# SSD decays from masked sums, norms applied to mixed rows, and experts' latent rows added by halves, in a hybrid diffusion kernel

## The chip, the cores and the metric

One core of a Trainium2 chip runs the whole program. The metric is the device time in microseconds from start to end of one execution, as a median of several runs.

The engines are TensorE (PE, with its weight loads PEld), VectorE (DVE), ScalarE (ACT), GpSimd (POOL) and SyncE (SP). Here SP does little but issue DMAs. POOL issues some as well, and each of these two issues its transfers in its own order.

## The reference

Two layers run over 512 latent tokens and 256 context tokens of 1024 features. Each layer is a mixer (attention beside a bidirectional Mamba-2 SSD) and then a mixture of 16 experts. In the first layer the context tokens go through both as well; in the second they give only keys, values and states. What matters for the change:

```python
# SSD, one direction; chunks of 128 tokens, 2 groups x 4 heads of 64 (xs, dt, a, bm, cm)
xdt  = xs * dt
a_cs = cumsum(dt * a)                                   # within a chunk
seg  = a_cs[target] - a_cs[source]
decay = exp(where(tri, seg, -inf))
y_diag = einsum(cb[target, source] * decay, xdt)        # cb = C . B, one for each group
...                                                     # + states carried from chunk to chunk
y = y_f + flip(y_b)
# norms that feed the output projection
ssd  = gated_group_rmsnorm(y + d_res * xs, z, ssd_norm_w)   # 2 groups of 256 features
attn = rmsnorm(o, subln_w) * (1.0 - lam_init)               # each of 4 heads, 128 features
mix  = concatenate([attn, ssd]) @ w_out
x = x + g1 * mix
# experts: each takes its 64 best latent rows (and, in layer 0, its 32 best context rows)
ye = (silu(xe @ w_gate) * (xe @ w_up)) @ w_down * gate
x = x + g2 * zeros(n, d).at[idx].add(ye)
```

## The kernel before

**Stages.** Tokens lie in six tiles of 128 rows: tiles 0 to 3 are latents, 4 and 5 context. A layer runs through the input norm, the projection of the SSD's inputs with their convolution and the SSD's first group, the gate projection with the SSD's second group, four attention heads, the output projection with the routing, and the experts. By time in the profile (us) the first layer has its SSD at 60 to 240, attention at 240 to 430, output projection and routing at 430 to 600, experts at 600 to 1262; the second starts at 1262 and has its SSD at 1330 to 1480, attention at 1480 to 1640, output projection and routing at 1640 to 1765, experts at 1765 to 2412.

**Products.** Matrix products of the mixer are made in three passes of rounded fp32: every operand is split into a high part (an ACT copy) and a low part (value less high part, on DVE or POOL). Weights arrive as `raw` tiles in a ring of four and are split into `rt` by the class with `pull` and `flush`; its next `raw` is loaded when a low part is done.

**Order.** The Python code interleaves generators. `Slots.tick` advances each of them to its next `yield`; work behind `yield STEP` is put in later in the same tick, between the other generators' pieces, and work behind a plain `yield` in the next tick. PE's projection matmuls fill the ticks. Each engine's queue is in that written order, as are SP's and POOL's DMA issues; no queue is reordered on the chip.

**An SSD chunk** (`chunk`) handles 128 tokens of four heads, both directions at once: 12 chunks in the first layer, 8 in the second. `acs` holds the cumulative sums with the source token on the partition. `dt_part` also transposes them and stores them in DRAM (`acsd`), and each chunk loads the four heads' rows back, repeated over all 128 partitions, as `RB` (128 x 2 directions x 4 heads x 128 targets, 512 KB). So `RB` less the source's `acs` is the exponent. The lower and upper triangles are taken by multiplying `cb` by 0/1 masks (`cbm`), and one exponential serves both directions, of the smaller of the two exponents:

```python
self.ld(RB..., src[None].to_broadcast([P, 2, 512]))                       # SP
nc.gpsimd.tensor_tensor(tf, RB[:, 0], a[:, 0]..., op=OP.subtract)          # POOL, L1057
nc.vector.scalar_tensor_tensor(tf[:, h], RB[:, 1, h], a[:, 1, h:h + 1], tf[:, h], subtract, min)   # L1068, four
nc.scalar.activation(E[:, h], cbm[:, 0], AF.Copy, scale=d[:, 0, h:h + 1])  # L1064, four
nc.vector.scalar_tensor_tensor(E[:, h], cbm[:, 1], d[:, 1, h:h + 1], E[:, h], mult, add)           # L1072, four
nc.scalar.activation(tf, tf, AF.Exp)                                       # L1069
nc.vector.tensor_tensor(E, E, tf, op=OP.mult)                              # L1074
```

(`E` is named `G` in the trace; `d` is dt.) PE then multiplies `E` by the inputs (`yd`, L1081) and adds the carried states' part (`yo`). `state` makes those, with POOL's `xd` and `hstep`.

**Norms.** `rsqrt_steps` is 11 small DVE steps for 1/sqrt, most of them behind a `yield STEP`. For each chunk of the second group `z_out` squares and sums both groups of the gated row on ACT, goes through `rsqrt_steps` (`yrs`), multiplies by the norm's weights `wssd` and stores the row to `mixd` in DRAM. `attend` does the same for one head and one tile with `ors` and `wsub` (L1837) and stores `ob`; for the last head's latent tiles it transposes `ob` in place instead. `op_in` loads a tile of mixed rows (`mixin`) back, transposes it and splits it into `mT`; `op_tile` multiplies it by `w_out` in `OUT_ORDER`, and adds to x.

**Experts.** SP streams each expert's weights without pause. `moe` makes `yl`, 128 partitions x 512, for an expert's 64 latent rows: partition 32*j + r and half g hold quarter j (256 columns) of row 32*g + r. `add_rows` multiplies each half by gate and `G2` into a `ys` of 128x256 and adds it to x in DRAM with an indirect DMA on POOL (L1666), 128 pieces of 1 KB, so twice for an expert's latents. The context's 32 rows are one more such scatter. x is `xr` in the first layer and `out` in the second.

Of the kernel before, what the change touches and what calls it, by code (L numbers as in the profile page):

```python
# [37 lines left out]
R_N1, R_N2, R_CW, R_CB, R_L = 0, 8, 16, 40, 48  # L38
# [26 lines left out]
OUT_ORDER = (4, 5, 6, 7, 0, 1, 2, 3)  # L65
# [47 lines left out]
class Pieces:  # L113
# [7 lines left out]
    def fetch(self):  # L121
        f = next(self.todo, None)
        if f:
            self.raw.append(f(self.net.rawp.tile([P, 512], F32, tag="raw", name="raw", bufs=4)))

    def pull(self, hi, lo):
        self.turn += 1
        nc, x = self.net.nc, self.raw.pop(0)
        nc.scalar.copy(hi.bitcast(F32R), x)  # L129
        self.flush()  # L130
        self.low = (nc.gpsimd if self.turn % 2 or x.shape[-1] == 384 else nc.vector), lo, x, hi

# [9 lines left out]
class Net:  # L142
# [122 lines left out]
    def consts(self, p1):  # L265
# [8 lines left out]
        for l in range(2):  # L274
# [96 lines left out]
    def pieces(self, l):  # L371
# [22 lines left out]

        cbs = [cb for g in range(2) for _, cb in GROUP[g]]
# [7 lines left out]
        for b in range(2):  # L403
            yield from (cols(w_out, k, 512 * b) for k in OUT_ORDER)

# [285 lines left out]
    def layer_params(self, l, lp, p1, lam_init):  # L691
# [7 lines left out]
        self.wsub = lp.tile([P, P], F32, name="wsub")  # L699
        self.wssd = lp.tile([P, 512], F32, name="wssd")  # L700
# [9 lines left out]
        ld(self.wsub, bc(I["subln_w"][l:l + 1], P))  # L710
        ld(self.wssd, bc(I["ssd_norm_w"][l:l + 1], 512))
# [6 lines left out]

        nc.vector.tensor_scalar(self.wsub, self.wsub, 1.0 - lam_init, None, op0=OP.mult)
# [152 lines left out]
    def dt_part(self, l, p1, sp, psp):  # L872
# [62 lines left out]
        nc.scalar.activation(self.eacs, self.acs, AF.Exp)  # L935
        yield
# [102 lines left out]
    def chunk(self, l, g, c, G, sp, yp):  # L1039
# [7 lines left out]
        a, d, ea = dgh(self.acs), dgh(self.dt), dgh(self.eacs)  # L1047
# [840 lines left out]
```

## Time and profile before

| what | before |
|---|---|
| median of 3 runs | 2430.44 us (2430.13 to 2430.88) |
| the profiled execution's own time | 2429.65 us |
| its span, first to last instruction | 2427.9 us |
| mean granted clock of TensorE, of full speed | 0.964 |
| PE busy | 2175.3 us, 90% of the span |
| DVE busy | 995.3 us, 41% |
| ACT busy | 635.9 us, 26% |
| POOL busy | 480.9 us, 20% |

The shares are means over stages that differ. The page's second part cuts the span into 40 slices of 60.7 us: DMA stands at 9 tenths in the expert stages, and at 2 to 3 in the first layer's SSD slices, where DVE is at 7 to 9. What a change in a stage can be worth is read there.

### The profile page before, as it was taken

How to read it: one execution, taken by the hardware profiler on the slowest of the kernel's cores; microseconds unless marked ns; L12 is line 12 of the kernel's file. 1: busy time of each engine (PE TensorE's matmuls, PEld its weight loads, DVE VectorE, ACT ScalarE, POOL GpSimd, SP SyncE). 2: the span in 40 equal slices, each digit the busy share in tenths (PEclk: the TensorE clock that was granted, in tenths of full speed). 3: DMA queues.
4: the chain of work that ended last, by engine and by line, in shares of the span. 5: the costliest groups of instructions: out<-in, count | busy, mean ns of one | idle time of the engine just before them, and what ended most of it. 6: DMA issues, size and time to landing. Idle time of an engine off the chain costs nothing. (4 is left out here: it accounts for less than half of the span.)

```text
span 2427.9 us, 55950 instructions
## 1 busy us (share of the span) xinstructions
PE 2175.3 (90%) x23460; PEld 1335.8 (55%) x23460; DVE 995.3 (41%) x3088; ACT 635.9 (26%) x1739; POOL 480.9 (20%) x584
## 2 busy tenths in 40 slices
PE   6898988998999999999987988989799999988775
PEld 4677787785445455455444667887543333333332
DVE  5789589873111111111116787887611111111010
ACT  4334467521111111111113443565111010101000
POOL 4464233100111101101103464241000001000001
PEclk9999999999999999999998998999899999999998
DMA  7322723678999999999994325324999999999997
GB/s 255 85 76 83 267 63 99 207 249 330 393 403 405 390 401 393 398 395 399 394 388 122 92 58 192 111 71 150 361 370 414 408 411 408 414 409 409 409 412 275
DMA packets 234759, 702.46 MB, mean 289 GB/s; under 512 B 30860, under 2 KB 88412, under 8 KB 234508
## 3 DMA queue, kind: packets, MB, share of 16 engines
q1 hardware_dynamic: 220428, 681.43, 72.6%
q0 software_dynamic: 14080, 17.46, 3.9%
q8 instruction: 185, 3.03, 0.5%
q14 instruction: 66, 0.54, 0.1%
HBM read 675.05 MB, written 23.76 MB: 288 GB/s over the span
## 5 line engine op out<-in xcount | busy, mean ns | idle before, releaser
L1490 PE MATMUL gl<-gw,xeT 128*32 128x512 f32 (+1 forms) x8192 | 655.6, 466 | 62.9 <-DMA gw<-w_up 62.7
L1490 PEld LDWEIGHTS gl<-gw,xeT 128*32 128x32 f32 x8192 | 277.7, 111 | 441.9 <-issue 404.3
L1529 DVE SCALAR_TENSOR_TENSOR th<-th,gl 128x256 f32<-128x256 f32 (+1 forms) x96 | 37.5, 391 | 702.9 <-ACT th L1528 702.9
L1536 PE MATMUL yl<-rt,hl 128*32 128x256 f32 x4080 | 247.5, 380 | 13.6 <-PE gl L1490 9.2
L1528 ACT ACTIVATE th<-gl 128x256 f32<-128x256 f32 (+1 forms) x96 | 35.1, 367 | 774.3 <-PE gl L1490 767.7
L171 PE MATMUL pacc<-rt,H 128*128 128x384 f32 (+1 forms) x768 | 206.3, 351 | 4.5 <-ACT V L1719 2.2
L1536 PEld LDWEIGHTS yl<-rt,hl 128*32 128x32 f32 x4080 | 134.1, 110 | 117.8 <-issue 16.0
L1666 POOL DMA_INDIRECT out<-ys,sidx x32 | 49.5, 1546 | 710.7 <-DVE ys L1665 599.1
L1665 DVE SCALAR_TENSOR_TENSOR ys<-yl,gate,G2l 128x256 f32<-128x256 f32 x64 | 28.0, 479 | 361.3 <-PE yl L1536 361.3
L1573 PE MATMUL gc<-gw,xeT 128*32 128x352 f32 x2048 | 170.6, 459 | 0.0
L171 PEld LDWEIGHTS pacc<-rt,H 128*128 128x128 f32 x768 | 137.8, 197 | 18.0 <-issue 6.3
L171 PE MATMUL xacc<-H,rt 128*128 128x512 f32 (+1 forms) x448 | 134.5, 376 | 6.8 <-ACT H L799 6.2
L171 PE MATMUL pacc<-rt,L 128*128 128x384 f32 (+1 forms) x384 | 130.0, 338 | 0.0
L1428 POOL DMA_INDIRECT xe<-xn2d,gidx x16 | 15.1, 944 | 529.4 <-PE xet L1438 389.8
L1443 ACT ACTIVATE xeT<-xet,MC,A 128x64 f32<-128x64 f32 (+1 forms) x256 | 74.3, 424 | 169.2 <-PE xet L1438 169.2
L137 POOL TENSOR_TENSOR rt<-raw,rt 128x384 fp32r<-128x384 f32 (+1 forms) x88 | 100.0, 1162 | 90.9 <-ACT rt L129 90.7
L171 PE MATMUL oacc<-woh,mT 128*128 128x512 f32 x304 | 107.2, 410 | 0.0
L1536 PE MATMUL yl<-wd,hl 128*32 128x256 f32 x1552 | 101.4, 382 | 4.4 <-DMA wd<-w_down 3.8
L1573 PEld LDWEIGHTS gc<-gw,xeT 128*32 128x32 f32 x2048 | 68.6, 110 | 56.2 <-issue 43.9
L171 PEld LDWEIGHTS xacc<-H,rt 128*128 128x128 f32 x448 | 82.2, 197 | 22.3 <-ACT H L799 7.0
L1666 POOL DMA_INDIRECT xr<-ys,sidx x32 | 49.9, 1560 | 194.9 <-DVE ys L1665 109.1
L1805 ACT ACTIVATE e<-sc,nm,rq 128x768 f32<-128x768 f32 (+1 forms) x80 | 72.1, 904 | 49.5 <-DVE nm L1801 46.9
(408 smaller groups left out, 3446.7 us busy)
## 6 DMA issues: line engine op xcount, KB each, us to landing
gw<-w_gate SPq DMA_DIRECT2D x256, 704.0 KB
gw<-w_up SPq DMA_DIRECT2D x256, 704.0 KB
rt<-w_down SPq DMA_DIRECT2D x255, 512.0 KB
wd<-w_down SPq DMA_DIRECT2D x97, 512.0 KB
mr<-w_mod SPq DMA_DIRECT2D x80, 512.0 KB
raw<-w_in SPq DMA_DIRECT2D x48, 256.0 KB
raw<-w_in SPq DMA_DIRECT2D x64, 192.0 KB
RB<-acsd SPq DMA_DIRECT2D x20, 512.0 KB
```

The lines of the kernel that those rows point to most:

```text
L137: e.tensor_tensor(lo.bitcast(F32R), x, hi, op=OP.subtract)
L171: self.nc.tensor.matmul(o, a[x].bitcast(F32R), b[y].bitcast(F32R), start=start and i == 0, stop=stop and i == 2, **kw)
L1428: self.nc.gpsimd.indirect_dma_start(out=xe[0:n], out_offset=None, in_=self.xn2d[0:rows], in_offset=bass.IndirectOffsetOnAxis(ap=idx[0:n, e ...
L1443: nc.scalar.activation(xT[:, kk, c:d], tr[:, k, c - a:d - a], AF.Identity, scale=self.A2[:, s, kk:kk + 1], bias=self.MC[:, l, s, 24 + kk:2 ...
L1490: self.nc.tensor.matmul(gl[c][32 * j:32 * j + 32, o:o + n].rearrange("p (u t i) -> p u t i", u=2, i=32), self.xT[:, k, 32 * g:32 * g + 32] ...
L1528: nc.scalar.activation(th, g, AF.Tanh, scale=0.5)
L1529: nc.vector.scalar_tensor_tensor(th, th, 1.0, g, op0=OP.add, op1=OP.mult)
L1536: nc.tensor.matmul(y[32 * j:32 * j + 32], h[:, b], wd[b][:, 256 * j:256 * j + 256], start=new and b == 0, stop=b == NF - 1, skip_group_che ...
L1573: nc.tensor.matmul(gc[u][32 * j:32 * j + 32].rearrange("p (t i) -> p t i", i=32), xT[:, k, 64:96], w, start=k == 0, stop=k == KD - 1, skip ...
L1665: nc.vector.scalar_tensor_tensor(ys, y, self.gate[:, i, e:e + 1], G2, op0=OP.mult, op1=OP.mult)
L1666: nc.gpsimd.indirect_dma_start(out=dst, out_offset=bass.IndirectOffsetOnAxis(ap=self.sidx[:, i, e:e + 1], axis=0), in_=ys, in_offset=None, ...
L1805: nc.scalar.activation(ei[:, 0:w], sc[:, i * w:i * w + w], AF.Exp, scale=rq[:, t, i:i + 1], bias=nm[:, i:i + 1], accum_out=sm[:, i:i + 1])
```

## The change

**SSD chunks.** `dt_part` computes `la` = ln(dt) in some 14 small DVE steps. In a chunk `RB` is first written with a mask (0 in the triangle, -1e30 outside) less the source's `acs`, the forward half on POOL, the backward half on DVE. The targets' sums are then added by a DMA that POOL issues, which adds into `RB`. Three ticks later ACT takes eight exponentials of 128x128 with `la` as bias, which gives dt times decay. DVE adds the two directions and multiplies by `cb` straight from PSUM. POOL's and DVE's `tf`, both `cbm`, the four ACT copies and DVE's `G` steps go.

**Norms.** `z_out` and `attend` leave the rows unscaled and store only the mean squares into `mss`, except for the last head's latent tiles. `op_in` makes one `rsqrt_steps` for all five or six norms of a tile and multiplies `mixin` on ACT piece by piece before the transposes. The norms' weights become factors of rows: of `w_out`'s last four blocks when these are split (`scaled`, `pull`), and of the transposed attention blocks (`head_split`). `OUT_ORDER` alternates the two kinds. In `attend` two small DVE steps go.

**Experts.** Partition 64*j + r of `yl` now holds half j (512 columns) of row r. `down_lat` has matmuls of 512 columns, half as many; one 128x512 multiply and one scatter of 128 pieces of 2 KB serve an expert's latents. Gates, indices and `G2` follow that layout. The context's scatter stays.

```diff
-OUT_ORDER = (4, 5, 6, 7, 0, 1, 2, 3)
+OUT_ORDER = (4, 0, 5, 1, 6, 2, 7, 3)
...
     def pull(self, hi, lo):
...
+        if scale is None or scale is False:
+            nc.scalar.copy(hi.bitcast(F32R), x)
+        else:
+            nc.scalar.activation(hi.bitcast(F32R), x, AF.Copy, scale=scale)
         self.flush()
-        self.low = (nc.gpsimd if self.turn % 2 or x.shape[-1] == 384 else nc.vector), lo, x, hi
+        pool = self.turn % 2 or x.shape[-1] == 384 if scale is None else scale is False
+        self.low = (nc.gpsimd if pool else nc.vector), lo, x, hi, scale
...
     def chunk(self, l, g, c, G, sp, yp):
...
         RB = sp.tile([P, 2, 4, P], F32, tag="RB", name="RB", bufs=2)
+        for i, e in enumerate((nc.gpsimd, nc.vector)):
+            e.tensor_tensor(RB[:, i], self.neg[:, i, None, :].to_broadcast([P, 4, P]), a[:, i, :, None].to_broadcast([P, 4, P]),
+                            op=OP.subtract)
...
-        self.ld(RB.rearrange("p d h q -> p d (h q)"), src[None].to_broadcast([P, 2, 512]))
-        yield
-        yield
+        nc.gpsimd.dma_start(RB.rearrange("p d h q -> p d (h q)"), src[None].to_broadcast([P, 2, 512]), accum_op=OP.add)
+        yield
+        yield
+        yield
+
+        for i in range(2):
+            for h in range(4):
+                nc.scalar.activation(RB[:, i, h], RB[:, i, h], AF.Exp, bias=la[:, i, h:h + 1])
+                if h % 2:
+                    yield STEP
...
+        nc.vector.tensor_tensor(E, RB[:, 0], RB[:, 1], op=OP.add)
+        yield
+        nc.vector.tensor_tensor(E, E, cb[:, None, :].to_broadcast([P, 4, P]), op=OP.mult)
...
     def z_out(self, l, t, ap):
...
-        rs = yield from self.rsqrt_steps(ap, ss, 2, 1.0 / 256, "yrs")
-        for g in range(2):
-            c = slice(256 * g, 256 * g + 256)
-            nc.vector.scalar_tensor_tensor(y[:, c], y[:, c], rs[:, g:g + 1], self.wssd[:, c], op0=OP.mult, op1=OP.mult)
+            nc.scalar.activation(junk, y[:, 256 * g:256 * g + 256], AF.Square, scale=1.0 / 16, accum_out=self.mss[:, t, g:g + 1])
         self.st(self.mixd[l][t * P:(t + 1) * P, 512:1024], y)
...
     def op_in(self, l, t, op, psp):
...
+        rs = yield from self.rsqrt_steps(op, self.mss[:, t, 0:n + 2], n + 2, 1.0, f"mrs{n}")
+        yield
+        cuts = [(512, 768), (768, D)] + [(P * h, P * h + P) for h in range(n)]
+        for i, (a, b) in enumerate(cuts):
+            nc.scalar.mul(mx[:, a:b], mx[:, a:b], rs[:, i:i + 1])
+            if i % 2:
+                yield STEP
...
+        def down_lat(y, h, wd, b):
+
+            for j in range(2):
+                for g in range(2):
+                    nc.tensor.matmul(y[64 * j + 32 * g:64 * j + 32 * g + 32], h[:, g, b], wd[b][:, 512 * j:512 * j + 512],
+                                     start=b == 0, stop=b == NF - 1, skip_group_check=True)
...
     def add_rows(self, mw, y, i, e, G2, dst):
         nc = self.nc
-        ys = mw.tile([P, 256], F32, tag="ys", name="ys", bufs=4)
-        nc.vector.scalar_tensor_tensor(ys, y, self.gate[:, i, e:e + 1], G2, op0=OP.mult, op1=OP.mult)
+        ys = mw.tile([P, 512 >> i], F32, tag=f"ys{i}", name="ys", bufs=2)
+        nc.vector.scalar_tensor_tensor(ys, y, self.gate[:, i, e:e + 1], G2[i], op0=OP.mult, op1=OP.mult)
...
     def attend(self, t):
...
-        nc.vector.tensor_tensor(nm, nm, nrq[:, t], op=OP.mult)
+        nc.vector.scalar_tensor_tensor(nm, nm, -1.0, rq[:, t], op0=OP.mult, op1=OP.mult)
...
+        own = self.h == 3 and not ctx
+        oss = ap.tile([P, 1], F32, tag="oss", name="oss", bufs=2) if own else n.mss[:, t, 2 + self.h:3 + self.h]
```

SP's queue in the first layer's SSD: `raw<-w_in` are projection weights, `acsd<-acsr` is the store of the cumulative sums. Before:

```order
L154 DMA raw<-w_in 128x512
L161 DMA acsd<-acsr 96x128
L154 DMA raw<-w_in 128x512
L154 DMA RB<-acsd 128x2x512 x4
L154 DMA raw<-w_in 128x512 x2
L154 DMA RB<-acsd 128x2x512
L154 DMA raw<-w_in 128x512
L154 DMA RB<-acsd 128x2x512
L154 DMA raw<-w_in 128x512 x2
L154 DMA RB<-acsd 128x2x512 x2
```

and after:

```order
L162 DMA raw<-w_in 128x512
L169 DMA acsd<-acsr 96x128
L162 DMA raw<-w_in 128x512 x7
L162 DMA raw<-w_in 128x3x128 x4
L162 DMA ropew<-q_norm_w 128x64
L162 DMA ropew<-k_norm_w 128x64
```

The `RB` loads, which had stood between the weights' loads, are gone from SP; they now stand on POOL, between its SSD steps (`xd`, `hstep`, `xD`) and the weights' low parts (`rt`):

```order
L1090 TENSOR_TENSOR RB<-neg,acs 128x512 x2
L1093 DMA RB<-acsd 128x2x512
L1054 TENSOR_TENSOR xd<-XS,te 128x256
L1045 TENSOR_TENSOR hstep<-H,etot 128x256
L1093 DMA RB<-acsd 128x2x512
L1051 TENSOR_TENSOR xd<-XS,te 128x512
L1110 TENSOR_TENSOR xD<-XS,Db 128x256
L143 TENSOR_TENSOR rt<-raw,rt 128x512
L1045 TENSOR_TENSOR hstep<-H,etot 128x256 x2
```

The first row is POOL's half of the masks of two chunks. A load stands right behind it, so it waits there for DVE's half, and the rows below it with it.

DVE around one chunk in the middle of the first layer's first SSD group, before:

```order
L1089 TENSOR_TENSOR Y<-yd,xD 128x256
L1068 SCALAR_TENSOR_TENSOR tf<-RB,acs,tf 128x128
L1092 TENSOR_TENSOR t_1432<-yo,eacs 128x512
L1059 TENSOR_TENSOR cbm<-cb,triu 128x128
L1060 TENSOR_TENSOR cbm<-cb,tril 128x128
L1068 SCALAR_TENSOR_TENSOR tf<-RB,acs,tf 128x128 x2
L1072 SCALAR_TENSOR_TENSOR G<-cbm,dt,G 128x128 x4
L1068 SCALAR_TENSOR_TENSOR tf<-RB,acs,tf 128x128 x2
L1074 TENSOR_TENSOR G<-G,tf 128x512
```

and after, where the three 128x512 steps of the chunks (`RB<-neg,acs`, `G<-RB`, `G<-G,cb`) stand among the convolution (`cv`) and one low part (`rt`):

```order
L1090 TENSOR_TENSOR RB<-neg,acs 128x512
L143 TENSOR_TENSOR rt<-raw,rt 128x512
L1019 SCALAR_TENSOR_TENSOR cv<-cv 128x770
L1108 TENSOR_TENSOR G<-G,cb 128x512
L1123 TENSOR_TENSOR Y<-yd,xD 128x256
L1106 TENSOR_TENSOR G<-RB 128x512
L1126 TENSOR_TENSOR t_1429<-yo,eacs 128x512
L1090 TENSOR_TENSOR RB<-neg,acs 128x512
L1108 TENSOR_TENSOR G<-G,cb 128x512
L1123 TENSOR_TENSOR Y<-yd,xD 128x256
```

Before, 12 of the 14 instructions shown are steps of the decay (`tf`, `cbm`, `G`), eight of them 128x128; after, five of ten are, all 128x512.

POOL at the end of the first layer's experts: `xr` are latents, `xc` context; the memsets of `cv` behind them belong to the second layer. Before, where the last expert's latents are two scatters:

```order
L1666 DMA xr<-ys,sidx_6125 2048x256
L1666 DMA xc<-ys,sidx_6125 1024x256
L1666 DMA xr<-ys,sidx_6125 2048x256 x2
L1666 DMA xc<-ys,sidx_6125 1024x256
L1666 DMA xr<-ys,sidx_6125 2048x256 x3
L959 MEMSET cv 128x1
```

and after, one scatter for an expert's latents, alternating with the context's:

```order
L1717 DMA xr<-ys,sidx_5634 1024x512
L1717 DMA xc<-ys,sidx_5634 1024x256
L1717 DMA xr<-ys,sidx_5634 1024x512
L1717 DMA xc<-ys,sidx_5634 1024x256
L1717 DMA xr<-ys,sidx_5634 1024x512
L997 MEMSET cv 128x1
```

Of the three last latents' scatters before the memsets, the last expert's two have become one.

## Rows read from the trace of the kernel before

**Rows 1.** Stages: length; PE, PEld, DVE, ACT, POOL busy; clock; DMA share; GB/s

```profile
60.00:240.00 180.00, 158.07 (x834) 127.40 (x833) 154.21 (x375) 72.17 (x186) 87.79 (x112) 0.92 0.27 78
240.00:430.00 190.00, 171.99 (x1204) 147.04 (x1203) 149.17 (x570) 113.17 (x322) 64.03 (x103) 0.96 0.42 143
430.00:600.00 170.00, 161.32 (x1253) 116.00 (x1254) 110.55 (x447) 53.71 (x148) 7.89 (x8) 0.96 0.75 261
600.00:1262.00 662.00, 644.68 (x9625) 331.70 (x9617) 91.93 (x228) 91.42 (x296) 83.39 (x59) 0.99 1.03 397
...
1330.00:1480.00 150.00, 127.50 (x705) 100.08 (x704) 127.29 (x288) 60.18 (x150) 77.49 (x103) 0.97 0.26 75
1480.00:1640.00 160.00, 143.67 (x1034) 128.49 (x1033) 123.83 (x419) 87.80 (x244) 60.12 (x97) 0.95 0.41 132
...
1765.00:2412.00 647.00, 572.79 (x7204) 245.55 (x7200) 80.54 (x246) 62.36 (x183) 46.38 (x30) 0.99 1.02 407
```

**Rows 2.** PE's waits in three stages: total us, times, longest us

```profile
PE yd L1081 <- DVE G L1074: 7.1, 3, 6.3
...
PE wtr L1824 <- DVE QL L1778: 6.4, 3, 3.2
PE mtr L1192 <- ACT wT L1825: 4.3, 1, 4.3
...
PE yd L1081 <- DVE yrs_y L215: 7.3, 1, 7.3
```

**Rows 3.** Chain at the end (start, us); timelines of POOL and SP

```profile
2413.75 3.88 DMA out<-ys,sidx
...
2418.38 1.54 POOL L1666 DMA_INDIRECT out<-ys,sidx  x1 [3.09 <-DMA out<-ys,sidx]
...
1279.53 1.57 POOL L1666 DMA_INDIRECT xr<-ys,sidx  x1 [27.19 <-DVE ys L1665]
1284.15 1.56 POOL L1666 DMA_INDIRECT xr<-ys,sidx  x1 [3.05 <-issue]
...
1288.17 1.75 SPq L154 DMA_DIRECT2D xin<-xr  x4
```

**Rows 4.** Groups by line: busy us, mean ns, idle before; one tile row: min/median/max ns

```profile
L1068 DVE SCALAR_TENSOR_TENSOR tf<-RB,acs,tf 128x128 f32<-128x128 f32 x80 | 38.3, 510 | 8.3 <-POOL tf L1057 8.3
...
L1072 DVE SCALAR_TENSOR_TENSOR G<-cbm,dt,G 128x128 f32<-128x128 f32 x80 | 37.3, 494 | 1.3 <-ACT G L1064 1.2
...
L1064 ACT ACTIVATE G<-cbm,dt 128x128 f32<-128x128 f32 x80 | 25.8, 390 | 22.3 <-DVE cbm L1059 22.3
...
L1837 DVE SCALAR_TENSOR_TENSOR ob<-ob,ors_y,wsub 128x128 f32<-128x128 f32 x40 | 19.6, 490 | 0.7
...
L1074 DVE TENSOR_TENSOR G<-G,tf 128x512 f32<-128x512 f32 x20 | 13.7, 683 | 0.1
...
L205 DVE TENSOR_TENSOR ors_e<-ors_e,ors_m 128x1 f32<-128x1 f32 x40 | 9.7, 243 | 0.7
...
L1068 DVE SCALAR_TENSOR_TENSOR tf<-RB,acs,tf x80: 334/341/1429, 93.2 to 1467.9; 128x128 f32<-128x128 f32 x80
```

**Rows 5.** Timelines of SP and POOL in the first layer: start, us, instruction, [idle before]

```profile
87.01 10.00 SPq L154 DMA_DIRECT2D RB<-acsd  x4
...
92.16 1.04 POOL L1057 TENSOR_TENSOR tf<-RB,acs 128x512 f32<-128x512 f32 x1 [2.31 <-DMA RB<-acsd]
...
134.04 1.64 POOL L1057 TENSOR_TENSOR tf<-RB,acs 128x512 f32<-128x512 f32 x1 [2.50 <-ACT cv L962]
...
42.96 0.54 POOL L158 DMA_DIRECT2D wssd<-ssd_norm_w  x1
```

**Rows 6.** DMA queues, 2040 to 2360 us: packets, MB, share of 16 engines

```profile
q1 hardware_dynamic: 29013, 128.62, 98.2%
q0 software_dynamic: 2304, 2.10, 4.1%
```

More of the change, by code (lines that the diff above doesn't have):

```diff
@@ L283, in consts @@
         self.lds(self.tril, I["k_tril"])
+        self.neg = cst.tile([P, 2, P], F32, name="neg")
+        for i, m in enumerate((self.triu, self.tril)):
+            nc.vector.tensor_scalar(self.neg[:, i], m, 1e30, -1e30, op0=OP.mult, op1=OP.add)
         self.cols = cst.tile([P, P], F32, name="cols")
@@ L403, in pieces @@
         for b in range(2):
-            yield from (cols(w_out, k, 512 * b) for k in OUT_ORDER)
+            yield from (scaled(cols(w_out, k, 512 * b), k - 4) if k > 3 else plain(cols(w_out, k, 512 * b)) for k in OUT_ORDER)
     def staged(self, W, ws, n, hi=None):
@@ L1507, in moe_open @@
         self.wp = self.tc.alloc_tile_pool(name=f"wd{l}", bufs=1, reuse_waits="tile", side="right")
-        self.G2 = [mw.tile([P, 256], F32, name="G2" + "lc"[s]) for s in range(2 if ctx else 1)]
+        self.G2 = [mw.tile([P, 512 >> s], F32, name="G2" + "lc"[s]) for s in range(2 if ctx else 1)]
         for s in range(2 if ctx else 1):
@@ L1530, in act, with down @@
             nc.vector.tensor_tensor(h, th, u, op=OP.mult)
-        def down(y, h, wd, b, new=True):
+        def down(y, h, wd, b):
             for j in range(4):
                 nc.tensor.matmul(y[32 * j:32 * j + 32], h[:, b], wd[b][:, 256 * j:256 * j + 256],
-                                 start=new and b == 0, stop=b == NF - 1, skip_group_check=True)
+                                 start=b == 0, stop=b == NF - 1, skip_group_check=True)
+        def down_lat(y, h, wd, b):
+            for j in range(2):
+                for g in range(2):
+                    nc.tensor.matmul(y[64 * j + 32 * g:64 * j + 32 * g + 32], h[:, g, b], wd[b][:, 512 * j:512 * j + 512],
+                                     start=b == 0, stop=b == NF - 1, skip_group_check=True)
         xe = None
@@ L1615, in moe @@
                 for b in range(NF):
-                    for g in range(2):
-                        down(y[:, 256 * g:256 * g + 256], hl[:, g], wd, b, g == 0)
+                    down_lat(y, hl, wd, b)
                     if ctx and not last and b > 3:
@@ L1622, in moe @@
                         xe = self.following(l, e, xe, nt)
-                for g in range(2):
-                    self.add_rows(mw, y[:, 256 * g:256 * g + 256], g, e, G2[0], dst[0])
+                self.add_rows(mw, y, 0, e, G2, dst)
                 if last:
```

143 lines of the change are left out of this document (77 added, 66 removed).

## The prediction

> **What bounds the kernel now.** I read the busy time by stage first [rows 1], then what TensorE (PE) waited for inside the stages [rows 2], then the last links of the chain of waits [rows 3]. The reader is to see two kinds of stage. In the two expert stages (600 to 1262 and 1765 to 2412) the DMA share is 1.02 to 1.03 at 397 to 407 GB/s: the weights' stream never pauses, so work saved on PE or VectorE (DVE) there is worth nothing, and only bytes, packets, or an earlier start of the stream count. In the mixers (60 to 600, 1330 to 1640) the DMA share is 0.26 to 0.75 and PE is the busiest engine, but not full: it idles 21.9 us of 180 in the first layer's SSD stage, 18.0 of 190 in its attention, 22.5 of 150 and 16.3 of 160 in the second layer's. DVE is 79 to 86% busy in these four. PE's longest waits there are on DVE, or on ScalarE (ACT) behind DVE [rows 2], and the granted clock is 0.92 to 0.97. That mean lies between the two levels 1.2 and 2.4 GHz: 0.92 says that 16% of the stage ran at 1.2. A mixer that ends earlier starts the next weights' stream earlier, so its gain reaches the end whole.
>
> **The sum is made against the profiled execution's own 2429.65 us (span 2427.9); the median of the three runs is 0.8 above it.**
>
> **SSD chunks.** 20 chunks lose, on DVE, four `tf` steps of 0.510, four `G` steps of 0.494 and one multiply of 0.683 [rows 4]: 4.7 us. They gain three 128x512 operations (the mask minus cumsum, the sum of the two directions, the product with cb), priced at the 0.683 of the same shape: 2.05 us. Net 2.65 us less for each chunk, 32 us in the first layer (12 chunks) and 21 in the second (8). ACT has eight exponentials of 128x128 where it had four copies and one exponential: at the 0.390 of such a copy 3.1 us a chunk, under a fifth of an engine that is 40% busy there [rows 1]; I charge nothing. POOL swaps its `tf` for a mask of the same shape, and issues the load: 0.54 us by the one POOL load of that size that has a row [rows 5].
>
> **The moved load.** Before, SyncE issued each `RB` load; it landed 5 us later (issued at 87.01, `tf` released at 92.16 [rows 5]). Now POOL issues it as an adding load, and its queue stands still until DVE's half of the mask is written; behind it are `xd`, `hstep` and the weights' lower halves, which PE needs. The chunk gives it three ticks before the exponentials. The six chunks of the first group have their `tf` from 92.16 to 134.04 [rows 5], 8.4 us apart, and they start two ticks apart; so three ticks are 12.6 us of slack. No row shows an adding load of 512 KB. Below, it costs what the plain load did (5 us); above, 256 packets of 2 KB at twice the 91 ns worked out below for an added packet of 1 KB are 2.9 us on 16 engines, on top of the 3.88 us that a small add takes to land [rows 3]: 7 us. Both fit in the slack. What I charge is the first chunk of each layer, where POOL now also waits for the store of the cumsums and for `ln(dt)`: 4 us a layer (0 to 8).
>
> When SyncE no longer waits for `RB` buffers its weight loads go out earlier; I take nothing for that. The mask on DVE and on POOL runs at the same moment. The trace shows what such company costs: `tf` on DVE took 0.510 on average where half of them took 0.341 or less (334 at least, 1429 at most [rows 4]). The Trainium skill (SBUF — State Buffer, "Who interferes with whom") states that a DVE instruction with two SBUF inputs and a GpSimd instruction that reads SBUF block each other, the second waiting for the whole of the first. By it a DVE mask would take up to 1.04 us more, 21 us over 20 chunks, and the sum for the chunks would be 32 instead of 53 us less; the long rows of `tf` agree that this happens.
>
> **Norms.** Every attention tile but the last head's latent ones (32 of 40), and all 10 SSD outputs, lose a chain of 11 small DVE steps, 0.243 for the one shown [rows 4], so at most 2.7 us, and a multiply of 0.490. About 16 tiles lie in the first attention stage: 51 us of DVE at most. In exchange 10 mixed tiles get one such chain each and five or six ACT multiplies of about 0.39, 2 us. The stores of `ob` and `Y` no longer sit behind the chain. The cost: PE's transposes of the first mixed tile now wait for ACT after the load landed; ACT's queue stops there, with attention's exponentials behind it. 2 us in each layer, +4.
>
> **What PE makes of it.** DVE falls to (154 - 32 - 16)/180 = 59% in the first SSD stage and (149 - 51)/190 = 52% in attention. One stage of this kernel already looks so: 430 to 600, DVE 65%, PE idle 5% at a clock of 0.96 [rows 1]. If the SSD stages come to that state, their PE work at full clock (158.1 - 14.4 = 143.7 and 127.5 - 4.5 = 123.0) takes 143.7/(0.95 x 0.96) = 157.6 and 134.9 us: 22.4 and 15.1 less. The attention stages would give 9.7 and 11.2 in the same way; I take half, since ACT ends waits there too (4.3 us in one row [rows 2]) and keeps its work: 10.5. The output projections and the routes behind them I leave as they are. Mixers: -48, bounds 0 and -58; with the +12 of the new waits, -36.
>
> **Latents' rows by halves.** An expert's two added scatters of 1 KB pieces become one of 2 KB pieces. At the end of the kernel the second is issued 4.63 us after the first, behind its landing [rows 3]; it goes, while one 128x512 multiply (0.683) stands where the first of two smaller stood, 0.2 later: -4.3 (-3.5 to -4.6). Between the layers the same pair (1279.53, 1284.15) holds SyncE's load of `xin` at 1288.17, and the second layer starts from that: -4.3 (-2 to -4.6). In the stream the queue of added packets took 4.1% of 16 engines over 320 us for 2304 packets, 91 ns each; the weights' took 173 ns for 4.4 KB, 39 ns a KB [rows 6]. An added packet of 2 KB then costs between 91 + 39 = 130 and 182 ns; 128 of them instead of 256 of 91 give 0 to 0.4 us for each expert, 0 to 12 over 30 experts in the stream. I take -6, the middle, since nothing shows which part of the 91 goes with bytes. PE's matmuls for it (half as many, twice as wide) lie under the stream: nothing.
>
> **Sum:** 2429.65 - 36 - 4.3 - 4.3 - 6 = 2379, and the median stands 0.8 higher: **2380 us**, 2.1% less.
>
> **Rivals.** (1) *PE's order, not DVE, holds the mixers.* For it: PE is busy for 601 of the four stages' 680 us, 88% [rows 1]. Against it: the releasers of its waits [rows 2]. Then only the two single scatters, some packets and a few us remain: 2410 to 2422. (2) *The mixers gain all of it*: DVE was late everywhere, no new wait shows, and the clock stays up: -58 and more, 2345 to 2362. (3) *The adding load is late* and the kernel ends slower. It sits on POOL's in-order queue; if an `RB` takes more than the 12.6 us of slack from its mask to its landing, the exponentials hold ACT, and DVE and PE behind it. Each us over costs up to 20 us; the saved 50 us are gone at 15 us, and 16 us would give 2380 + 20 x 3.4 = 2448. Against it: the 5 to 7 us above. The Trainium skill (DMA: Bandwidth & Descriptors, "Anatomy of one DMA") puts a load issued by GpSimd at 2.0 us and its bytes at 436 GB/s: 3.2 us for 512 KB, an estimate by that page; no row here shows an adding load. (4) *The change does less than it says*: ACT takes over as the engine that is late in attention (113 of 190 us busy now), and the packets of 2 KB cost double; no gain outside the SSD stages, 2424 to 2434.
>
> **Chances.** Forecast, 2362 to 2405: 0.62. Rival 1: 0.17. Rival 2: 0.11. Rival 3: 0.06. Rival 4: 0.04. To leave out no more than a fifth the range reaches into rivals 1 and 2: 2350 to 2420. A measurement of this kernel tells 0.2%, 4.9 us, from no change; faster by more than that 0.90 (forecast, rivals 1 and 2), within it 0.04, slower 0.06.
>
> **What would show it.** In the changed profile: one scatter after the last multiply, its end under 10 us behind the last matmul; `xin` loads some 4 us sooner after the last expert's matmuls; DVE under 65% and PE idle near 5% in the SSD and attention stages; no wait of PE's `yd` on a norm chain; the expert stages as long as now or some us shorter at a higher GB/s. I am wrong if POOL shows long waits at the adding load, if ACT shows waits on `RB`, or if DVE gets emptier in the mixers while PE's idle time stays.

## The result, and where the time went

The changed kernel takes 2405.67 us (2403.08 to 2406.82, 4 runs) where the kernel before took 2430.28 (2428.93 to 2430.88, 4 runs): a ratio of 0.9898, interval 0.9883 to 0.9914. That is 24.6 us or 1.0% less; 50 were forecast. The profiled execution took 2405.83, span 2404.1, granted clock 0.967.

Where did the other half go? The program's own landmarks tell it. Each layer runs its PE groups in one order: `xacc` (the SSD inputs' projection, with the first SSD group beside it), `zacc` (the gate projection, second SSD group), `pacc` (the heads' projection, attention), `oacc` (output projection). The second layer before, by tile (count: min/median/max ns, first and last start in us, shapes):

```profile
L171 PE MATMUL xacc<-H,rt x224: 276/393/794, 1311.2 to 1412.7; 128*128 128x512 f32 x64, 128*128 128x256 f32 x48
L171 PE MATMUL zacc<-rt,H x64: 392/396/1415, 1419.2 to 1453.1; 128*128 128x512 f32 x64
L171 PE MATMUL pacc<-rt,H x384: 277/336/1167, 1453.6 to 1632.9; 128*128 128x384 f32 x128, 128*128 128x256 f32 x64
L171 PE MATMUL oacc<-woh,mT x112: 387/393/774, 1645.1 to 1734.6; 128*128 128x512 f32 x112
```

and after:

```profile
L179 PE MATMUL xacc<-H,rt x224: 276/392/799, 1296.7 to 1413.5; 128*128 128x512 f32 x64, 128*128 128x256 f32 x48
L179 PE MATMUL zacc<-rt,H x64: 388/397/799, 1415.1 to 1452.2; 128*128 128x512 f32 x64
L179 PE MATMUL pacc<-rt,H x384: 277/336/682, 1454.0 to 1612.0; 128*128 128x384 f32 x128, 128*128 128x256 f32 x64
L179 PE MATMUL oacc<-woh,mT x112: 390/397/774, 1626.9 to 1715.5; 128*128 128x512 f32 x112
```

From the first `xacc` to the last the second layer takes 101.5 us before and 116.8 after: 15.3 more. From the last `zacc` to the last `pacc` it takes 179.8 and 159.8: 20.0 less. The same distances for both layers, and for two of the experiments below:

| stretch (us) | before | after | old decays | plain load, DVE masks |
|---|---|---|---|---|
| layer 1, first to last `xacc` | 124.7 | 130.7 | 123.9 | 116.4 |
| to the last `zacc` | 54.0 | 55.7 | 51.6 | 51.2 |
| to the last `pacc` | 204.7 | 186.5 | 189.5 | 180.5 |
| to the first `oacc` | 13.6 | 15.7 | 15.9 | 15.8 |
| layer 2, first to last `xacc` | 101.5 | 116.8 | 102.0 | 106.2 |
| to the last `zacc` | 40.4 | 38.7 | 42.0 | 37.9 |
| to the last `pacc` | 179.8 | 159.8 | 166.0 | 159.0 |
| to the first `oacc` | 12.2 | 14.9 | 14.8 | 14.4 |

So the SSD stretches (to the last `zacc`) lost 21.3 us and the attention stretches gained 38.2: 16.9 for mixers that were forecast to gain 36 (48 less 12 for new waits). (The forecast's SSD stages end some 30 us later, at 240 and 1480, so the stretches are not its terms; the experiments measure those.) Windows laid on these landmarks show the state of the engines: `xacc` to `zacc` and `zacc` to `oacc` of the first layer, then of the second, before (columns as in rows 1):

```profile
30.00:208.00 178.00, 157.96 (x908) 121.89 (x908) 146.84 (x310) 71.70 (x175) 92.73 (x122) 0.92 0.33 93
208.00:427.00 219.00, 194.05 (x1306) 166.82 (x1305) 174.89 (x660) 121.85 (x348) 76.23 (x119) 0.94 0.40 136
1311.00:1453.00 142.00, 126.52 (x682) 96.65 (x681) 120.42 (x233) 61.23 (x138) 71.10 (x91) 0.99 0.26 76
1453.00:1645.00 192.00, 165.72 (x1159) 148.54 (x1157) 153.84 (x541) 101.76 (x285) 74.48 (x115) 0.93 0.41 131
```

and after:

```profile
32.00:218.00 186.00, 162.35 (x907) 123.93 (x908) 135.24 (x219) 80.15 (x217) 107.30 (x132) 0.91 0.38 83
218.00:420.00 202.00, 188.01 (x1309) 164.65 (x1308) 137.89 (x396) 121.14 (x349) 76.89 (x120) 0.97 0.45 147
1297.00:1452.00 155.00, 130.19 (x678) 100.62 (x678) 122.72 (x201) 69.36 (x171) 83.94 (x102) 0.94 0.32 71
1452.00:1627.00 175.00, 159.90 (x1162) 142.98 (x1160) 125.76 (x352) 101.31 (x282) 71.54 (x114) 0.97 0.44 142
```

In the attention stretches DVE fell from 174.9 to 137.9 us and from 153.8 to 125.8, and PE's idle time with it: 25 to 14 us, and 26 to 15. In the SSD stretches DVE is emptier too in the first layer (146.8 to 135.2), but PE idles 24 us instead of 20, and in the second 25 instead of 15, at a clock of 0.94 where it had been 0.99; there DVE's busy time did not even fall (120.4 and 122.7, for 233 and 201 instructions). DVE stands at 73 and 79% of the SSD stretches and at 68 and 72% of the attention's, where the prediction's sign was under 65%. That is the mark that the prediction named for its own failure: a smaller share of DVE, PE idle all the same. One such place, from the timelines of POOL, ACT, DVE and PE in the second layer (start, us, instruction, idle before it and its releaser):

```profile
1360.46 1.31 POOL L1093 DMA_DIRECT2D RB<-acsd  x1
...
1372.12 1.21 POOL L1093 DMA_DIRECT2D RB<-acsd  x1 [0.30 <-POOL RB L1090]
...
1366.54 0.99 ACT L1100 ACTIVATE RB<-RB,la 128x128 f32<-128x128 f32 x3 [7.71 <-DMA RB<-acsd]
1367.43 0.56 ACT L1000 COPY cv<-xacc 128x512 f32<-128x512 f32 x1
...
1372.24 0.36 ACT L1000 COPY cv<-xacc 128x256 f32<-128x256 f32 x1
...
1377.42 2.15 ACT L1100 ACTIVATE RB<-RB,la 128x128 f32<-128x128 f32 x7 [3.51 <-DMA RB<-acsd]
1379.48 0.83 ACT L1017 ACTIVATE cv<-cv 128x770 f32<-128x770 f32 x1
...
1372.98 0.73 DVE L1011 TENSOR_SCALAR cv<-cv,cw 128x770 f32<-128x770 f32 x1
...
1377.69 1.01 DVE L1015 SCALAR_TENSOR_TENSOR cv<-cv,cw 128x770 f32<-128x770 f32 x1
...
1380.76 0.95 DVE L1019 SCALAR_TENSOR_TENSOR cv<-cv 128x770 f32<-128x770 f32 x1
...
1381.77 1.54 PE L1026 MATMUL xtr<-ident,cv 128*128 128x128 f32 x6 [5.65 <-DVE cv L1019]
```

POOL issues an adding load at 1360.46. ACT reaches its exponentials early and stands 7.71 us until the bytes are there. Behind these in its queue lie the copies of `xacc` for the convolution (`cv`, L1000): they come at 1367.43 and 1372.24, 5.5 and 3.6 us after PE had finished the sums (1361.90 and 1368.66). So DVE starts the convolution at 1372.98, its last step has its turn at 1380.76, between DVE's other steps, and PE's transpose waits for that: 5.65 us. ACT's next wait, 3.51 us for the load issued at 1372.12, cost little here: it takes seven exponentials before the convolution's tanh (L1017), but the tanh had its input only when L1015 ended, at 1378.70, and so lost 0.8 us at most. The whole account of `RB` (tile rows as above, then what ACT's wait was put down to, then the time from issue to landing):

```profile
L1100 ACT ACTIVATE RB<-RB,la x160: 382/388/412, 103.0 to 1437.9; 128x128 f32<-128x128 f32 x160
L1090 POOL TENSOR_TENSOR RB<-neg,acs x20: 1030/1090/1751, 91.5 to 1427.4; 128x512 f32<-128x512 f32 x20
L1090 DVE TENSOR_TENSOR RB<-neg,acs x20: 681/1095/2125, 96.3 to 1427.0; 128x512 f32<-128x512 f32 x20
L1093 POOL DMA_DIRECT2D RB<-acsd x20: 1192/1205/1741, 97.5 to 1429.4; - x20
...
  DMA RB<-acsd: 58.1, 15
...
DMA to landing us min/median/max: 5.2/5.4/8.3
```

ACT waited at 15 of the 20 chunks, 58.1 us. What DVE's convolution waited in turn for ACT's copies in the first layer's SSD, 60 to 215 us, before (total, times, longest):

```profile
DVE cv L973 <- ACT cv L962: 4.2, 4, 1.7
```

and after:

```profile
DVE cv L1011 <- ACT cv L1000: 17.5, 6, 5.6
```

In the second layer's SSD stretch that wait is no longer than before (4.9 and 5.0 us); there DVE stands at the sum of the two directions instead (before, its `G` waited 0.6 us for ACT):

```profile
DVE G L1106 <- ACT RB L1100: 4.8, 2, 3.6
```

The latents' side went as forecast. At the end there is one scatter; the chain has one link where [rows 3] had two, and the span ends 11.3 us after the last matmul (2392.8) instead of 15.0 (2412.9), though not under the 10 that the prediction named. `xin` is loaded 6.7 us after the last `yl` starts, instead of 10.1. The timelines of SP and POOL at these two places, after:

```profile
1273.41 2.73 SPq L162 DMA_DIRECT2D xin<-xr  x4
...
2393.90 1.55 POOL L1717 DMA_INDIRECT out<-ys,sidx  x1 [41.91 <-DVE ys L1716]
```

The queue of added packets in the second layer's stream, 2016 to 2336 us (packets, MB, share of 16 engines):

```profile
q0 software_dynamic: 1152, 2.10, 3.5%
```

1152 packets take 3.5% of 16 engines over 320 us, 156 ns each, where [rows 6] gave 91 for a packet of half the size.

### The profile page after: what moved, and what is told of

Its sections match the earlier page's. It is cut to its first block, busy times and chain, and to the rows that moved or that the text cites. A ratio compares the mean times of both kernels' runs of the same rounds, so it can differ in the third digit from the quotient of the medians.

```text
span 2404.1 us, 49640 instructions
## 1 busy us (share of the span) xinstructions
PE 2186.4 (91%) x20620; PEld 1253.2 (52%) x20620; DVE 911.8 (38%) x2460; ACT 663.7 (28%) x1851; POOL 459.0 (19%) x574
## 5 line engine op out<-in xcount | busy, mean ns | idle before, releaser
L1589 PE MATMUL yl<-rt,hl 128*32 128x512 f32 x2040 | 257.5, 595 | 9.6 <-PE gl L1535 9.2
L1716 DVE SCALAR_TENSOR_TENSOR ys<-yl,gate,G2l 128x512 f32<-128x512 f32 x32 | 24.0, 751 | 380.9 <-PE yl L1589 380.9
L1717 POOL DMA_INDIRECT out<-ys,sidx x16 | 24.9, 1558 | 731.3 <-DVE ys L1716 590.4
L179 PE MATMUL xacc<-H,rt 128*128 128x512 f32 (+1 forms) x448 | 140.7, 390 | 7.0 <-ACT H L820 6.6
L179 PEld LDWEIGHTS pacc<-rt,H 128*128 128x128 f32 x768 | 133.4, 190 | 21.6 <-POOL rt L143 10.5
L1589 PEld LDWEIGHTS yl<-rt,hl 128*32 128x32 f32 x2040 | 69.2, 109 | 142.3 <-issue 87.9
L1589 PE MATMUL yl<-wd,hl 128*32 128x512 f32 x776 | 102.0, 599 | 2.7 <-DMA wd<-w_down 2.1
L179 PE MATMUL xacc<-L,rt 128*128 128x512 f32 (+1 forms) x224 | 83.2, 373 | 3.0 <-POOL L L883 2.6
L1502 PE MATMUL xpk<-x,one 128*64 128x512 f32 x256 | 82.0, 634 | 3.4 <-DVE one L1498 3.4
```

Of the source, the lines that this page charges most:

```text
L179: self.nc.tensor.matmul(o, a[x].bitcast(F32R), b[y].bitcast(F32R), start=start and i == 0, stop=stop and i == 2, **kw)
L1502: nc.tensor.matmul(ps[64 * j:64 * j + 64], one[:, t], self.x1[t][:, 512 * j:512 * j + 512], start=t == 0, stop=t == NL - 1, skip_group_che ...
L1589: nc.tensor.matmul(y[64 * j + 32 * g:64 * j + 32 * g + 32], h[:, g, b], wd[b][:, 512 * j:512 * j + 512], start=b == 0, stop=b == NF - 1, s ...
L1717: nc.gpsimd.indirect_dma_start(out=dst[i], out_offset=bass.IndirectOffsetOnAxis(ap=self.sidx[:, i, e:e + 1], axis=0), in_=ys, in_offset=No ...
```

## Experiments

All times are medians, the ratios against runs of the kernel before on the same chip (2429.4 to 2431.4). Runs of one kernel lie up to 9 us apart, so 2 or 3 us tell nothing.

**Parts apart.** First, the changed kernel with the SSD chunks of before (`dt_part` without `la`):

```diff
-        nc.gpsimd.dma_start(RB.rearrange("p d h q -> p d (h q)"), src[None].to_broadcast([P, 2, 512]), accum_op=OP.add)
+        self.ld(RB.rearrange("p d h q -> p d (h q)"), src[None].to_broadcast([P, 2, 512]))
...
-        nc.vector.tensor_tensor(E, RB[:, 0], RB[:, 1], op=OP.add)
+        nc.gpsimd.tensor_tensor(tf, RB[:, 0], a[:, 0, :, None].to_broadcast([P, 4, P]), op=OP.subtract)
...
```

> The changed kernel with the SSD chunks of before (plain RB load on SyncE, tf, cbm, G); norms deferred and latents' rows by halves stay. Theory 1, the adding load is late: in the changed trace the projection of the first SSD group took 6 us more than before in the first layer and 15 us more in the second, while the attention stages took 18 and 20 us less; without the new chunks the 21 us come back and the attention keeps its gain, 2378 to 2392 us. Rival, the attention is quicker because the chunks left less behind for it: 2405 to 2420.

2391.37, ratio 0.9834 (0.9818 to 0.9851). The new chunks cost 14.3 us; without them the SSD stretches are as before and the attention keeps 29.0 of its 38.2 us (third column of the table). Then the chunks alone, their part of the diff on the kernel before:

```diff
+        self.neg = sp.tile([P, 2, P], F32, name="neg")
...
         self.la = la = sp.tile([P, NT, 16], F32, name="la")
```

> The kernel before with the SSD chunks of the change alone (masks, adding load, eight exponentials, ln(dt)); the masks are made per layer because of space. Theory 1: about 21 us slower than before, 2440 to 2455. Rival (the new chunks gain, as predicted from DVE's busy time): 2385 to 2410.

2443.56, ratio 1.0051 (1.0034 to 1.0068): 12 us slower than before, less than the 21 that were expected, since the stretches behind give 7.3 back. `RB` waits there as in the changed kernel (66.6 us, 16 times). The latents alone, which is `down_lat`, `add_rows` and what goes with them:

```diff
-                for g in range(2):
-                    self.add_rows(mw, y[:, 256 * g:256 * g + 256], g, e, G2[0], dst[0])
+                self.add_rows(mw, y, 0, e, G2, dst)
```

> The kernel before with the latents' rows by halves alone. Theory: the two last scatters bring 4.3 us each and the stream about 4 us (the landmarks of the changed trace show 3.8 us less in the two expert stages), so 2415 to 2421 against 2430.3 to 2431.4 before. Rival, the packets of 2 KB bring nothing in the stream: 2421 to 2423; rival, they bring the 6 us or more of the prediction: under 2416.

2416.76, ratio 0.9948 (0.9931 to 0.9964): -12.7. In this run's own trace the span ends 10.4 us after the last matmul and `xin` is loaded 7.0 us after the last `yl` starts, so the end and the load bring 4.6 and 3.1, which leaves 5.0 for the stream. Last, on the kernel with the old chunks, the SSD rows' norms put back as well:

```diff
-            nc.scalar.activation(junk, y[:, 256 * g:256 * g + 256], AF.Square, scale=1.0 / 16, accum_out=self.mss[:, t, g:g + 1])
+            nc.scalar.activation(junk, y[:, 256 * g:256 * g + 256], AF.Square, accum_out=ss[:, g:g + 1])
+        yield
+        rs = yield from self.rsqrt_steps(ap, ss, 2, 1.0 / 256, "yrs")
...
-        cuts = [(512, 768), (768, D)] + [(P * h, P * h + P) for h in range(n)]
+        cuts = [(P * h, P * h + P) for h in range(n)]
```

> The changed kernel with the SSD chunks of before and also the SSD rows' norms of before (z_out with its chain of small steps and wssd); attention's norms deferred, latents' rows by halves. Theory, attention's norms bring nearly all of what the deferral brings: 2391 to 2399 (2391.4 with both deferred). Rival, PE's waits of yd for the z_out chain (2.1 and 7.3 us before) were the larger part: 2400 to 2415.

2395.06, ratio 0.9853 (0.9831 to 0.9875). `z_out`'s share is 3.7 us, within the runs' spread; the attention's norms and small steps are worth 2416.8 - 2395.1 = 21.7.

**What of the chunk is late.** The same wide steps with a plain load, first on SyncE's queue, then on POOL's:

```diff
-        for i, e in enumerate((nc.gpsimd, nc.vector)):
-            e.tensor_tensor(RB[:, i], self.neg[:, i, None, :].to_broadcast([P, 4, P]), a[:, i, :, None].to_broadcast([P, 4, P]),
-                            op=OP.subtract)
...
-        nc.gpsimd.dma_start(RB.rearrange("p d h q -> p d (h q)"), src[None].to_broadcast([P, 2, 512]), accum_op=OP.add)
+        self.ld(RB.rearrange("p d h q -> p d (h q)"), src[None].to_broadcast([P, 2, 512]))
         yield
         yield
+        for i, e in enumerate((nc.gpsimd, nc.vector)):
+            e.tensor_tensor(RB[:, i], RB[:, i], self.neg[:, i, None, :].to_broadcast([P, 4, P]), op=OP.add)
         yield
```

(`dt_part` takes `acs` from `la` once; the second kernel has `nc.gpsimd.dma_start` for `self.ld`.)

> The changed kernel, but RB is a plain load on SyncE's queue at the start of the chunk, as before; POOL and DVE add the masks to it two ticks later, the source's sums go into the exponential's bias, the exponentials come at the same tick as now. The same wide steps on each engine, only the adding DMA and its place on POOL are gone. Theory 1: the first SSD groups take no longer than before the change, 2370 to 2390. Rival (the wide steps on DVE and POOL stand in each other's way, or the exponentials load ACT too much): 2400 to 2410.

> As the run before, but the plain load is issued by POOL instead of SyncE, at the same place in the program. If the adding itself (packets that cost more, and a load that must wait for the masks) makes the SSD late: within 4 us of the run with SyncE. If it is POOL's queue, behind whose other steps the load is issued: 2395 to 2410.

2387.99, ratio 0.9818 (0.9801 to 0.9834), and 2400.88, ratio 0.9872 (0.9856 to 0.9889). Of the 17.7 us that the plain load on SyncE brings, 12.9 go when POOL issues it, and 4.8 more, within the spread, when it adds (the masks then stand ahead of the load instead of behind it). So most of it comes with the issue by POOL. Two things that come with it were not taken apart: the load's place behind POOL's other steps, and long steps on DVE. In the SSD stages no step of DVE takes over 2.2 us in any kernel whose `RB` load SyncE issues; in each of the five kernels here whose load POOL issues, 4 to 9 do, four of them in the changed kernel (2.27, 4.05, 5.56 and 4.62 us). Where a kernel with POOL's load has one with SyncE's beside it, DVE is busy 1.6 to 13.4 us longer in the former. But 2388.0 is only 3.4 less than with the old chunks, with all their DVE steps: something else still held the new ones. Next, one tick more between load and exponentials, with three `RB` buffers, once for each kind of load:

```diff
         yield
+        yield
         for i in range(2):
             for h in range(4):
                 nc.scalar.activation(RB[:, i, h], RB[:, i, h], AF.Exp, bias=la[:, i, h:h + 1])
```

> The changed kernel with one more tick between the adding load and the exponentials, and three RB buffers in place of two. ACT waited 58 us for RB in the changed trace. Theory, the load lands later than three ticks give it: a tick more takes most of that wait, 2388 to 2398. Rival, POOL's queue and not the distance is late, so the exponentials find the load late again: 2401 to 2410.

> The kernel with the plain load on SyncE and masks after it, with one more tick between the masks and the exponentials, and three RB buffers in place of two. There ACT still waited for POOL's masks (26 us in the first layer's SSD). Theory, that wait is what is left of the SSD's loss: 2374 to 2384. Rival, PE and the ticks' order hold the stage and the wait is beside the path: 2385 to 2392.

2397.65, ratio 0.9868 (0.9847 to 0.9889): 8 us less with the adding load, the upper edge of the first theory, but ACT still waits 52.5 us for it. 2385.90, ratio 0.9820 (0.9799 to 0.9841): 2 us less with the plain one, nothing. There the two masks run at the same moment, and ACT waits for the later, POOL's:

```profile
L1095 DVE TENSOR_TENSOR RB<-RB,neg x20: 676/1154/1774, 93.9 to 1405.1; 128x512 f32<-128x512 f32 x20
L1095 POOL TENSOR_TENSOR RB<-RB,neg x20: 1261/1657/2016, 94.1 to 1401.9; 128x512 f32<-128x512 f32 x20
...
  POOL RB L1095: 29.2, 14
```

One step of 128x512 takes DVE 1154 ns in the median, against 676 at least, and POOL 1657 against the 1042 of the `tf` step of that shape before. So both masks went to DVE, first with the plain load and then with the adding one:

```diff
-        for i, e in enumerate((nc.gpsimd, nc.vector)):
+        for i, e in enumerate((nc.vector, nc.vector)):
```

> The kernel with the plain load, masks after it and one tick more, both masks on DVE instead of one on POOL: 0.68 us of DVE more in a chunk, one POOL step of 1.3 to 1.6 us less in a queue that PE's xd waits for. If POOL's queue is the late one in what is left of the SSD: 2376 to 2383. If the two engines only trade: 2384 to 2390.

> The changed kernel with its adding load, one more tick before the exponentials, three RB buffers, and both masks on DVE: the counterpart of the kernel with the plain load, masks on DVE and one tick more (2369.8), differing from it only in the load. If POOL's mask step is what the change lost and the adding load is harmless once it has its tick: 2368 to 2375. If the adding load on POOL's queue still costs what it cost beside POOL's mask (2397.7 against 2385.9 with four ticks, 12 us): 2379 to 2386. If it is worse without company: over 2388.

2369.81, ratio 0.9752 (0.9735 to 0.9768): 16.1 us less, with 0.7 us more of DVE's work in each chunk, and below the 2376 to 2383 that were expected. It is the quickest kernel so far, 60.8 us under the one before. With the adding load 2386.63, ratio 0.9819 (0.9802 to 0.9835): 16.8 us more, though it has its tick and POOL's queue is free of masks. The two compared on `RB` by tile, first with the plain load (masks, then what ACT's wait was put down to):

```profile
L1095 DVE TENSOR_TENSOR RB<-RB,neg x40: 678/746/1817, 95.5 to 1393.6; 128x512 f32<-128x512 f32 x40
...
  DVE RB L1095: 18.0, 14
```

then with the adding one:

```profile
L1090 DVE TENSOR_TENSOR RB<-neg,acs x40: 671/726/2602, 94.7 to 1406.2; 128x512 f32<-128x512 f32 x40
...
  DMA RB<-acsd: 56.9, 15
```

Masks take 746 and 726 ns in the median; what differs is ACT's wait, 18.0 us for DVE against 56.9 for the DMA, and six steps of DVE of 2.2 to 3.1 us with POOL's load. Last, why POOL's half of the mask cost 16 us. In the best kernel POOL got a step back that nobody reads, once an addition of the mask's shape, once a memset:

```diff
+        jk = sp.tile([P, 4, P], F32, tag="jk", name="jk", bufs=1)
+        nc.gpsimd.tensor_tensor(jk, self.neg[:, 0, None, :].to_broadcast([P, 4, P]), self.neg[:, 0, None, :].to_broadcast([P, 4, P]), op=OP.add)
         for i, e in enumerate((nc.vector, nc.vector)):
```

```diff
+        jk = sp.tile([P, 1024], F32, tag="jk", name="jk", bufs=1)
+        nc.gpsimd.memset(jk, 0.0)
         for i, e in enumerate((nc.vector, nc.vector)):
```

> The kernel with the plain load, both masks on DVE and one tick more (2369.8), and where POOL's mask step stood POOL adds two tiles of the same shape, which nobody reads and which waits for no load. If a POOL step there costs by itself (its place in POOL's queue, or the company of DVE's steps), most of the 16 us between the two places of the mask come back: 2380 to 2390. If the 16 us came from the exponentials' wait for POOL's half: 2368 to 2375.

> The same with a memset of 128x1024 on POOL instead, which reads nothing. If POOL's time in the queue is what costs: as much for each us of POOL as in the run with the added step, so near it when the memset takes about as long. If what costs is POOL and DVE reading at once: 2368 to 2375, with DVE's steps no longer stretched.

2381.04, ratio 0.9808 (0.9791 to 0.9825), 11.2 us more; and 2366.71, ratio 0.9745 (0.9728 to 0.9761), 3.1 less, which is nothing. The added step itself by tile, the addition:

```profile
L1095 POOL TENSOR_TENSOR jk<-neg x20: 1033/1366/1754, 89.2 to 1354.6; 128x512 f32<-128x512 f32 x20
```

and the memset:

```profile
L1095 POOL MEMSET jk<- x20: 947/950/953, 88.6 to 1342.8; 128x1024 f32 x20
```

950 ns of POOL's queue, placed ahead of `xd` and `hstep`, cost nothing, so it isn't a microsecond of POOL's time. The addition takes anything from 1033 to 1754 and costs 11.2 us; the memset, which reads nothing, is never stretched (947 to 953). DVE is busy 913.4 us without the step, 921.5 with the addition and 911.3 with the memset. The larger part of the 16 us thus goes with two engines that read at once; the rest, up to 5 us, may be the exponentials' wait for POOL's half, which no run took apart.

**Is DVE's time the bound at all?** DVE's work was put back, with results that nobody reads: in each chunk of the kernel with the plain load and one tick more, where the four steps stand ahead of `E`'s product with `cb` and so put that off too, and in `attend` of the kernel with the old chunks, behind the store.

```diff
         nc.vector.tensor_tensor(E, RB[:, 0], RB[:, 1], op=OP.add)
+        jk = sp.tile([P, 512], F32, tag="jk", name="jk", bufs=1)
+        for i in range(4):
+            nc.vector.tensor_tensor(jk, E.rearrange("p h q -> p (h q)"), E.rearrange("p h q -> p (h q)"), op=OP.mult)
+            yield STEP
```

```diff
         n.st(n.mixd[self.l][t * P:(t + 1) * P, P * self.h:P * self.h + P], ob)
+        jr = yield from n.rsqrt_steps(ap, oss, 1, 1.0, "ors")
+        jk = ap.tile([P, P], F32, tag="jk", name="jk", bufs=1)
+        nc.vector.scalar_tensor_tensor(jk, ob, jr, ob, op0=OP.mult, op1=OP.mult)
```

> The kernel with the plain load, masks after it and one tick more, and in every chunk four multiplies of 128x512 more on DVE, whose result nobody reads: at the 0.683 of such a step 2.7 us a chunk, 55 us of DVE in the two SSD stages, as much as the change was to save there. If DVE's busy time is what holds the SSD stages, as the prediction had it, 2410 to 2440 (2385.9 without them). If PE's order and the waits hold them: 2384 to 2395.

> The kernel with norms deferred and the SSD chunks of before, and in every attention tile that defers its norm DVE's chain of 11 small steps and one 128x128 multiply again, into tiles that nobody reads: DVE is as busy as before the deferral, but no store and no transpose waits for the chain. If DVE's time is what the deferral gave back: 2405 to 2416 (2391.4 without the steps). If it was the wait for the chain: 2390 to 2397.

2412.64, ratio 0.9922 (0.9901 to 0.9942): 26.7 us more for 80 steps of 0.688, 55 us. 2409.21, ratio 0.9917 (0.9900 to 0.9935): 17.8 more of the 21.7 that the deferral had brought. So in attention it was DVE's time and not a wait for the chains. A microsecond of DVE put there is worth 0.49 us in the SSD stages, and 17.8/(32 x 3.0) = 0.19 in attention (11 steps of 0.243 [rows 4] and one of 0.352).

## Why the prediction missed

The time lies inside the range, and the direction was right. The forecast's 50 us were twice the 24.6 measured, and the forecast's own band of 2362 to 2405 ends 0.7 us below the measured time. By parts, forecast and measured: chunks, their load and `z_out` -29.5 and +10.6 (14.3 less 3.7); attention's norms with `op_in` -6.5 and -21.7; latents -14.6 and -12.7. So one term was 40 us too good, one 15 us too bad.

- **What bounds the kernel: right in the main.** The expert stages follow the stream, DVE's time costs PE's in the mixers, and a mixer's gain reaches the end. Rival 1 (PE's order alone) falls with the two runs that load DVE. Two slips in the readings carry nothing: DVE's lowest share in the four stages is 77% (123.8 of 160), not 79, and the exponentials of 12 chunks at 3.1 us are 21% of the first SSD stage.
- **The SSD stages: wrong, by 40 us.** Three steps of the working failed.
  - *The relief itself.* 53 us of DVE were to go with the chunks. In the whole program DVE is busy 932.8 us with the old chunks and 911.8 with the new ones: 21 went. The 60 wide steps, priced at 0.683, took 51.5 us, 0.86 each; the 32 small steps of `ln(dt)`, charged at nothing, took 11.4; and other steps grew (the convolution's L1013 1.75 us in the mean, 1.17 before). Both `cbm`, 11.1 us that also went, were not counted.
  - *"If the SSD stages come to that state"* took DVE as all that holds them: the 53 us, and `z_out`'s chains, were to bring 37.5. At 0.49 the 53 would have been worth 26, and the 21 are worth 10. The best kernel shows 21.6 less than the old chunks, with 19.4 us off DVE; what brings the rest there, no run took apart.
  - *"Both fit in the slack"* failed most. The load's own price was right (5.4 us in the median, within 5 to 7), though its issue holds POOL 1.2 us and not 0.54, which was read from a load of 256 KB, half of `RB`'s. The slack of 12.6 us was not there: it counted three ticks at the chunks' pace, 4.2 us each, from the mask on, but POOL issues the load behind its other steps and after DVE's half, and ACT runs ahead of that pace. In the changed trace the bytes are there 8.9 us in the median after POOL's mask starts (7.0 to 14.2), and ACT stands at the exponentials 6.1 us after it. The charge of 8 us stands against 12 to 18 measured (11.8 with four ticks and POOL's mask, 16.8 with DVE's, 17.7 with three ticks), in which DVE's long steps have a part. Rival 3 had the mechanism, ACT held and DVE and PE behind it, but not its threshold: it was to cost from a lateness of 12.6 us on, and cost well below that. For the chunks alone its sign came true, 0.5% slower than before.
- **Masks on two engines at once: charged at nothing, cost 11 to 16.** The row of `tf` was in hand, 0.510 in the mean against a median of 0.341. The rule quoted from the Trainium skill (SBUF — State Buffer, "Who interferes with whom") gave 21; the runs agree with its kind and with half to three quarters of its size. The same section of the Trainium skill says that a DVE instruction with two SBUF inputs is not hindered by a GpSimd instruction that only writes; the memset run agrees (2366.7, 947 to 953 ns).
- **Attention: right in kind, too small.** 10.5 were forecast from DVE's relief, and 21.7 came with `op_in`'s cost already paid. "I take half, since ACT ends waits there too" is the step that failed: DVE's time was nearly all of it (17.8 us when the steps were put back), and PE's idle time and its clock gained together, 25 to 14 us idle and 0.94 to 0.97 in the first layer's stretch.
- **`op_in`: right.** +4 forecast for the wait of the transposes; the stretch from the last `pacc` to the first `oacc` grew by 2.1 and 2.7.
- **Latents: right.** 14.6 forecast, 12.7 measured: 4.6 and 3.1 for 4.3 each, 5.0 for 6. An added packet of 2 KB costs 156 ns, between the bounds 130 and 182.

## What to carry to other kernels

Before work is taken off a busy engine, look at what the replacement puts into a queue ahead of someone else: here a load that one in-order engine issues behind its own steps and that another waits for cost 12 to 18 us, most of the 21.6 that the new chunks bring without it and without the split mask. Count too what the replacement itself adds: of 53 us that were to come off DVE, 21 did. Slack is to be read from when the waiting engine gets there, not from the pace of the loop. And a step split between VectorE and GpSimd, at the same moment and both reading, can be slower than the two halves one after the other on VectorE.

## What the runs showed of the hardware

An adding load of 512 KB issued by POOL lands 5.4 us after its issue (5.2 to 8.3); its 2 KB packets take 22.3% of 16 engines in 80 us for 1632 of them, 175 ns each (second layer's SSD, all of that queue's packets):

```profile
q0 software_dynamic: 1632, 3.15, 22.3%
```

POOL is held 1.2 us by each issue (1192 to 1741 ns), and 0.73 by that of a plain load of the same bytes (730 to 807). One convolution step of DVE, 1.02 us in the median, took 5.56 while a load that POOL had just issued was under way:

```profile
1399.60 1.20 POOL L1093 DMA_DIRECT2D RB<-acsd  x1
...
1400.60 5.56 DVE L1013 SCALAR_TENSOR_TENSOR cv<-cv,cw 128x770 f32<-128x770 f32 x1
```

The three other long steps of the changed kernel (2.27, 4.05 and 4.62 us) also began 0.6 to 3.5 us after such an issue, with the load under way. No kernel without `RB` loads on POOL shows any in its SSD stages; no run shows why.
